# A masked softmax on one core: SyncE's first store waits for one more step of VectorE

## Chip, cores and metric

The kernel runs on one core of a Trainium2 chip. The metric is the device time of one execution in microseconds (us); the median of 3 runs of the kernel before is 156.31 us (156.23 to 156.35).

## What is computed

```python
def setup_inputs():
    batch, heads, seq_q, seq_k = 16, 8, 256, 256
    return {
        "x": np.random.randn(batch, heads, seq_q, seq_k).astype(np.float32),
        "lengths": np.random.randint(seq_k // 2, seq_k, size=batch).astype(np.int32),
    }

def reference(x, lengths):
    result = np.zeros_like(x)
    for b in range(batch):
        length = lengths[b]
        masked = x[b, :, :, :length].copy()
        masked = masked - np.max(masked, axis=-1, keepdims=True)
        exp_masked = np.exp(masked)
        result[b, :, :, :length] = exp_masked / np.sum(exp_masked, axis=-1, keepdims=True)
    return result.astype(np.float32)
```

It is a softmax over the last axis in which the columns from `lengths[b]` on are left out and come back as zeros. The input and the output are 33.55 MB each.

## The kernel before

**Tiles and slots.** One batch is one tile: 128 partitions with 16 rows (nt) of 256 columns each, 16 KB in a partition, 2 MB in all. SBUF holds 8 slots of this size (xt). There are 16 positions; positions 0, 1 and 2 hold batches 1, 2 and 3, position 3 holds batch 0, and from 4 on position and batch are the same (batch_of).

**Loads.** Position 0 is loaded from SyncE's queue in two halves (L136). Positions 1 and 2 are loaded whole from GpSimd's queue (L182). From position 3 on, GpSimd reads the batch's length into a register and picks the narrowest of some fixed widths that holds it (pick, L154): a narrow load, whose rows are 160 to 240 columns wide, or a whole one. Columns from 160 on were filled with zeros beforehand in the slots that get narrow loads (fill, L177). From position 4 on this is a loop, and a load there waits until the load two positions before has landed and until the slot's old tile is stored; so GpSimd has at most two of these loads out at a time.

**Compute.** For a tile, VectorE masks the columns from 128 on by a minimum with a ramp (mask, clip, L237; it raises the semaphore s_min), ScalarE does the exponential with the row's sum, 8 rows for each half tile (rows, L344; s_exp), and VectorE divides each half: a reciprocal of the 128x8 sums (L258) and a multiply (divide, L261; s_out). VectorE's order is written out by hand: both half masks of position 0, then for each position b the division of the first half, the mask of position b+1, the division of the second half. For b = 1 the mask of position 2 comes ahead of both divisions. So s_min is 2 after the two half masks of position 0, and 3 after the mask of position 1, which stands directly behind the division of the first half of position 0.

**Stores.** SyncE issues all stores in order (L143), in halves, quarters or whole tiles (parts). Each waits for the divisions that it covers (s_out); from position 2 on the first store of a position also waits until the stores of two positions before have landed (s_st).

**The end.** Behind the last division VectorE checks the row sums and TensorE counts the bad ones. With this input none is, and a second pass with subtracted maxima (L356 on) isn't run.

Of the kernel before, what the change touches and what calls it, by code (L numbers as in the profile page):

```python
# [21 lines left out]
def kernel(  # L22
# [6 lines left out]
    nc = tc.nc  # L29
# [18 lines left out]
    def batch_of(pos):  # L48
        return pos + 1 if pos < ahead else 0 if pos == ahead else pos
# [7 lines left out]
    def parts(b):  # L57


        if b == 0:  # L60
            cuts = [0, half, nt]
        elif b < 8:
            cuts = [0, half, half + quarter, nt]
        elif b < 13 or b == batch - 1:
            cuts = [0, half, nt]
        else:
            cuts = [0, nt]
        return [slice(i, j) for i, j in zip(cuts, cuts[1:])]
# [30 lines left out]
    with tc.tile_critical(no_gpsimd_drain=True):  # L99
# [11 lines left out]
        s_min = sem("s_min")  # L111
# [22 lines left out]
        for h in range(2):  # L134
            s = slice(h * half, (h + 1) * half)
            nc.sync.dma_start(out=xt[:, 0, s], in_=x_f[batch_of(0), :, s]).then_inc(s_ld[h], 16)  # L136
        for b in range(batch):
            s_b = s_st[b % 2]
            for s in parts(b):
                nc.sync.wait_ge(s_out, 2 * b + (s.stop - 1) // half + 1)  # L140
                if b >= 2 and s.start == 0:
                    nc.sync.wait_ge(s_b, 64 * (b // 2 + 1))
                nc.sync.dma_start(  # L143
                    out=out_f[batch_of(b), :, s, :], in_=xt[:, b % slots, s, :]
                ).then_inc(s_b, 16 * ((s.stop - s.start) // quarter))
# [262 lines left out]
```

## Time and profile before

| | |
|---|---|
| median of 3 runs | 156.31 us (156.23 to 156.35) |
| profiled execution: its time, its span | 156.43 us, 154.7 us |
| VectorE busy | 116.9 us (76%) |
| ScalarE busy | 105.5 us (68%) |
| GpSimd busy | 22.6 us (15%) |
| moved by DMA | 61.57 MB, 398 GB/s over the span |
| share of the 16 DMA engines | SyncE's queue (q1) 56.0%, GpSimd's (q0) 42.1% |
| HBM | 27.98 MB read, 33.55 MB written |

The span runs from the first to the last instruction; the time of the execution is 1.7 us longer. The DMA shares are the time that packets took, over 16 engines times the span. Engines are named as in the profile: DVE is VectorE, ACT is ScalarE, POOL is GpSimd, SP is SyncE; a small q behind a name is the engine's own queue of instructions that it issues. In the trace each DMA packet has a queue, a start, a duration and a size.

### The profile page before, as it was taken

The page shows a single profiled execution, that of the slowest core. Times are in us where ns is not written, and L with a number is a line of the kernel's source. Part 1 is how long each engine was busy: PE and PEld are TensorE (multiplying, and loading weights), DVE is VectorE, ACT ScalarE, POOL GpSimd, SP SyncE. Part 2 cuts the span into 40 slices and gives each one's busy share as a digit, 9 for nine tenths or more (in the row PEclk, how much of TensorE's full clock was granted, in tenths as well). Part 3 has the DMA queues.
Part 4 walks back from the last instruction along what each step waited for, and adds up shares of the span by engine and source line. Part 5 has one row for each costly group of instructions (what it writes and reads, how often), then busy time and mean ns, then how long its engine had stood idle before and what let it go on. Part 6 is the DMA issues. An engine that isn't in the chain of part 4 may idle for free.

```text
span 154.7 us, 1304 instructions
## 1 busy us (share of the span) xinstructions
PE 0.3 (0%) x2; PEld 0.2 (0%) x2; DVE 116.9 (76%) x91; ACT 105.5 (68%) x514; POOL 22.6 (15%) x30
## 2 busy tenths in 40 slices
PE   0000000000000000000000000000000000000000
PEld 0000000000000000000000000000000000000000
DVE  1349769996969696979979696969697686968500
ACT  3096889749595959688695959595968829596000
POOL 4994000100220200202030020220010000000000
DMA  4999999999999999999999999999999999999992
GB/s 121 420 430 436 273 420 416 379 410 441 414 401 391 423 406 421 409 415 421 393 421 410 411 415 401 419 411 421 415 419 417 437 430 415 432 447 415 434 417 95
DMA packets 10357, 61.57 MB, mean 398 GB/s; under 512 B 866, under 2 KB 978, under 8 KB 6642
## 3 DMA queue, kind: packets, MB, share of 16 engines
q1 hardware_dynamic: 5616, 35.65, 56.0%
q0 software_dynamic: 4736, 25.89, 42.1%
q14 instruction: 3, 0.02, 0.1%
q10 hardware_dynamic: 2, 0.00, 0.0%
HBM read 27.98 MB, written 33.55 MB: 398 GB/s over the span
## 4 chain that ended last, share of the span: by engine, by line
DMA 43%; DVE 29%; ACT 10%; issue 7%; ACTq 3%; POOL 1%; POOLq 1%; SPq 0%; PE 0%
DMA xt<-in_x_dram 23%; DMA out_dram<-xt 19%; DVE xt L261 15%; DVE xt L237 12%; ACT xt L344 10%; ACTq L344 3%; DVE inv_sum L258 1%; POOL xt L177 1%; DMA word<-in_lengths_dram 1%; DVE ends L293 0%; ACTq L350 0%; POOLq L126 0%; SPq L143 0%; DVE bad L296 0%; DVE len_s L228 0%
## 5 line engine op out<-in xcount | busy, mean ns | idle before, releaser
L344 ACT ACTIVATE xt<-xt (+1 forms) x256 | 102.4, 402 | 34.4 <-DVE xt L237 34.4
L261 DVE TENSOR_TENSOR xt<-xt,inv_sum 128x2048 f32<-128x2048 f32 x32 | 73.4, 2292 | 1.1
L344 ACT ACTIVATION_READ_ACCUMULATOR xt<-xt (+1 forms) x256 | 47.9, 187 | 0.0
L237 DVE SCALAR_TENSOR_TENSOR xt<-down,len_s,xt 128x2048 f32<-128x2048 f32 (+1 forms) x17 | 37.8, 2221 | 9.0 <-DMA xt<-in_x_dram 9.0
L154 POOL DMA_DIRECT2D xt<-in_x_dram x13 | 13.8, 1065 | 89.5 <-DMA out_dram<-xt 50.7
L258 DVE RECIPROCAL inv_sum<-row_sum 128x8 f32<-128x8 f32 x32 | 6.4, 199 | 15.9 <-ACT xt L344 15.9
L177 POOL MEMSET xt<- 128x1536 f32 x5 | 6.7, 1400 | 1.1 <-DVE len_s L228 1.1
L337 ACT ACT_TABLE_LOAD x1 | 1.3, 1283 | 1.6 <-SPq L99 1.6
L220 DVE TENSOR_SCALAR down<-iota_i 128x256 f32<-128x256 int32 x1 | 0.3, 301 | 1.6 <-POOL iota_i L167 1.6
L182 POOL DMA_DIRECT2D xt<-in_x_dram x2 | 1.2, 606 | 0.0
L293 DVE TENSOR_REDUCE ends<-row_sum 128x1 f32<-128x256 f32 x2 | 0.7, 411 | 0.0
L207 PE MATMUL count<-bad,ones_c 128*1 128x3 bf16 x1 | 0.2, 165 | 142.5 <-DVE bad L296 142.5
L225 DVE CAST len_b<-word 1x16 bf16<-1x16 int32 x1 | 0.2, 165 | 0.4 <-DMA word<-in_lengths_dram 0.4
L228 DVE TENSOR_SCALAR len_s<-len_f 128x16 f32<-128x16 f32 x1 | 0.2, 175 | 0.4 <-PE len_f L205 0.4
L167 POOL IOTA iota_i<- 128x256 int32 x1 | 0.3, 332 | 0.6 <-SPq L99 0.6
L304 DVE TENSOR_REDUCE redo<-count 1x1 f32<-1x3 f32 x1 | 0.1, 149 | 0.3 <-PE count L207 0.3
L296 DVE TENSOR_SCALAR bad<-ends 128x1 bf16<-128x1 f32 x3 | 0.3, 149 | 0.0
L173 POOL MEMSET seed<- 1x1 f32 x2 | 0.2, 226 | 0.0
L207 PEld LDWEIGHTS count<-bad,ones_c 128*1 128x1 bf16 x1 | 0.1, 79 | 142.6 <-DVE bad L296 142.6
L337 ACT ACTIVATE warm<-const-float32-0.0 128x1 f32<-128x1 f32 x1 | 0.2, 203 | 0.0
L170 POOL MEMSET ones<- 1x128 bf16 x1 | 0.2, 195 | 0.0
L205 PE MATMUL len_f<-len_b,ones 1*128 1x16 bf16 x1 | 0.2, 168 | 2.6 <-DVE len_b L225 2.6
(8 smaller groups left out, 0.8 us busy)
## 6 DMA issues: line engine op xcount, KB each, us to landing
out_dram<-xt SPq DMA_DIRECT2D x21, 1024.0 KB
xt<-in_x_dram POOLq DMA_DIRECT2D x4, 2048.0 KB, 14.3
out_dram<-xt SPq DMA_DIRECT2D x14, 512.0 KB
xt<-in_x_dram POOLq DMA_DIRECT2D x3, 1728.0 KB, 16.3
out_dram<-xt SPq DMA_DIRECT2D x2, 2048.0 KB
xt<-in_x_dram POOLq DMA_DIRECT2D x2, 1600.0 KB, 19.1
xt<-in_x_dram POOLq DMA_DIRECT2D x2, 1280.0 KB, 14.0
xt<-in_x_dram SPq DMA_DIRECT2D x2, 1024.0 KB, 6.4
```

Source lines behind the costliest of these rows:

```text
L154: nc.gpsimd.dma_start(out=xt[:, slot, :, :w], in_=x_n[:, b, :, :w]).then_inc(s_sw[par], 16)
L167: nc.gpsimd.iota(iota_i, pattern=[[1, seq_k]], base=0, channel_multiplier=0).then_inc(s_iota, 1)
L177: nc.gpsimd.memset(xt[:, b, :, low:], 0.0).then_inc(s_fill, 1)
L182: nc.gpsimd.dma_start(out=xt[:, b], in_=x_f[batch_of(b)]).then_inc(s_ld[b + 1], 16)
L207: nc.tensor.matmul(count, lhsT=ones_c, rhs=bad, start=True, stop=True).then_inc(s_count, 1)
L220: nc.vector.tensor_scalar(out=down, in0=iota_i, scalar1=0.5, scalar2=-big, op0=ALU.add, op1=ALU.mult)
L237: return nc.vector.scalar_tensor_tensor(out=t, in0=down[:, None, lo:hi].to_broadcast([P, s.stop - s.start, hi - lo]), scalar=len_s[:, batc ...
L258: step(nc.vector.reciprocal(out=inv_sum[:, b, s], in_=row_sum[:, b, s]))
L261: nc.vector.tensor_tensor(out=t, in0=t, in1=inv_sum[:, b, s, None].to_broadcast([P, half, seq_k]), op=ALU.mult,).then_inc(s_out, 1)
L293: step(nc.vector.tensor_reduce(out=ends[:, k : k + 1], in_=values, op=op, axis=AX))
L337: nc.scalar.activation(out=warm, in_=nc.const_aps.tensor(0.0, (P, 1), F32), func=EXP)
L344: ins = nc.scalar.activation(out=e, in_=e, func=EXP, accum_out=sum_h[:, i, j])
```

## The change

SyncE waits once, after the two loads of position 0 that it issues and ahead of its loop over stores, until s_min is at least 3, which is when VectorE has masked the tile of position 1. Nothing else is changed: the loads, whole and narrow, stay in GpSimd's queue, and each engine's instructions are the same and in the same order.

```diff
         for h in range(2):
             s = slice(h * half, (h + 1) * half)
             nc.sync.dma_start(out=xt[:, 0, s], in_=x_f[batch_of(0), :, s]).then_inc(s_ld[h], 16)
+        nc.sync.wait_ge(s_min, 3)
         for b in range(batch):
             s_b = s_st[b % 2]
             for s in parts(b):
```

## The prediction

> **What bounds the kernel now.** I read the page first, for the engines against the transfers. SyncE, VectorE and ScalarE all sit idle in every part of the span; the 16 DMA engines do not.
>
> ```profile
> span 154.7 us, 1304 instructions
> PE 0.3 (0%) x2; PEld 0.2 (0%) x2; DVE 116.9 (76%) x91; ACT 105.5 (68%) x514; POOL 22.6 (15%) x30
> DMA  4999999999999999999999999999999999999992
> GB/s 121 420 430 436 273 420 416 379 410 441 414 401 391 423 406 421 409 415 421 393 421 410 411 415 401 419 411 421 415 419 417 437 430 415 432 447 415 434 417 95
> ```
>
> The row of nines says that the DMA engines have work from the second slice to the last but one. The row below it says that the work goes at nearly one pace (400 to 440 GB/s), with one hole: the fifth slice (15.5 to 19.3 us), at 273 GB/s, while the busy digit stays at 9. In that slice the packets are slow, not missing. So this kernel ends when 61.57 MB have been moved. An edit that only reorders waits changes the time only by what it does to the pace of the packets, or by making the DMA engines run dry.
>
> Second, the view of stretches, cut where the pace changes (the last two columns are the DMA share and GB/s):
>
> ```profile
> 4.00:13.00 9.00, 0.00 (x0) 0.00 (x0) 4.61 (x4) 5.41 (x27) 8.11 (x8) 1.00 1.02 426
> 13.00:15.00 2.00, 0.00 (x0) 0.00 (x0) 1.85 (x2) 1.18 (x6) 0.45 (x1) 1.00 1.04 442
> 15.00:19.00 4.00, 0.00 (x0) 0.00 (x0) 3.37 (x3) 2.79 (x14) 0.72 (x1) 1.00 0.99 297
> 21.00:27.00 6.00, 0.00 (x0) 0.00 (x0) 5.93 (x5) 5.39 (x29) 0.00 (x0) 1.00 1.02 418
> 27.00:29.00 2.00, 0.00 (x0) 0.00 (x0) 1.97 (x3) 2.00 (x12) 0.00 (x0) 1.00 1.01 348
> 31.00:130.00 99.00, 0.00 (x0) 0.00 (x0) 82.92 (x58) 74.75 (x369) 10.94 (x10) 1.00 1.02 415
> 130.00:152.00 22.00, 0.17 (x1) 0.08 (x1) 13.31 (x16) 9.69 (x48) 0.00 (x0) 1.00 0.99 420
> ```
>
> Two slow stretches stand out, both with full queues. Stretch 1 (15 to 19) costs 4 x (1 - 297/426) = 1.21 us; stretch 2 (27 to 29) costs 2 x (1 - 348/418) = 0.33 us.
>
> Third, what happens just before them, in the timeline (SyncE, VectorE, GpSimd) and the DMA queues of short windows (q0 is GpSimd's queue with the loads, q1 SyncE's with the stores; packets, MB, share of the 16 engines):
>
> ```profile
> 13.48 5.32 SPq L143 DMA_DIRECT2D out_dram<-xt  x2
> 13.61 2.35 DVE L237 SCALAR_TENSOR_TENSOR xt<-down,len_s,xt 128x2048 f32<-128x2048 f32 x1 [0.15 <-DMA xt<-in_x_dram]
> 14.55 1.16 POOL L154 DMA_DIRECT2D xt<-in_x_dram  x1 [2.20 <-issue]
> 20.71 2.35 DVE L237 SCALAR_TENSOR_TENSOR xt<-down,len_s,xt 128x2048 f32<-128x2048 f32 x1 [2.31 <-DMA xt<-in_x_dram]
> ```
>
> ```profile
> q0 software_dynamic: 60, 0.88, 103.8%
> ...
> q0 software_dynamic: 30, 0.44, 75.4%
> q1 hardware_dynamic: 14, 0.11, 13.5%
> ...
> q0 software_dynamic: 174, 0.70, 101.2%
> q1 hardware_dynamic: 3, 0.00, 0.1%
> ```
>
> These are the windows 13 to 15, 17 to 19 and 27 to 29. In the packet records the first store, issued at 13.48, has a single packet before 17.8 and flows steadily only from 19. From 15.2 until then the loads' 16 KB packets, which took 0.61 us each before, take 1.0 to 1.3 us. In stretch 2 the pattern comes back: q1 has run dry at 26.9, the next store was issued at 25.53 (behind a multiply that ends at 25.50), its first packet runs at 29.0, and the loads' 4.8 KB packets take about 1.2 times their usual 0.19 us until then. So each time a store starts on an idle q1, the loads slow down from about 1.7 us after its issue to 3.5 to 5.6 us after it: by 30% (297 against 426) while a whole load is running, by 17% (348 against 418) while a narrow one is. Elsewhere q1 always has a backlog and there is no such stretch.
>
> **The change part by part.** One wait of SyncE is added, for s_min at 3. VectorE works in order: the first multiply of the first tile (which lets the first store go), then the mask of the second tile, which raises s_min to 3. That mask runs from 13.61 for 2.35 us, so the wait is over at 15.96 and the first store goes at about 15.99 in place of 13.48: 2.5 us later. The wait itself costs tens of ns, on an engine that only issues. Since the mask always stands behind that multiply, the wait cannot be met early; the change does what it says.
>
> What is queued behind it: all other stores. The second waits for a multiply that ends at 18.40, and is issued at 18.43, so it is not moved. Who waits for the first store: SyncE's first store of the third tile (issued at 30.41; the first tile's stores have landed by 27.95, 2.4 us of cover) and GpSimd's reuse of the first slot (load issued at 52.48, 24 us of cover). Both stay covered. What the DMA engines do in between: q0 holds the rest of the third tile's whole load, the fourth tile's narrow load (1.5 MB) and from 14.55 another narrow one (1.6 MB), over 8 us of work. They don't run dry. So the delay itself costs nothing; if that cover were gone it would cost up to 2.5 us.
>
> What it moves is the start-up of q1. Slowing begins 1.7 us after the issue: 17.7. The third tile's 2.1 MB start to flow at about 13.1 and need 4.9 us at 426 GB/s; undisturbed, they are through at about 18.0 to 18.5. So of the new stretch 0.3 to 0.8 us fall on the whole load (30%: 0.1 to 0.25 us), and the rest, until 3.5 to 5.6 us after the issue (19.5 to 21.6), on the narrow load (1.2 to 3.1 us at 17%: 0.2 to 0.5 us). The sum is 0.3 to 0.75 us; I take 0.5, since the end lies between two equally near rows. Against 1.21 this saves 0.7 us (0.45 to 0.9).
>
> Then stretch 2. The third tile now lands near 19.0 in place of 20.7, so its mask (at 20.71 after an idle 2.31) comes 1.7 us earlier, and the two multiplies behind it too, since ScalarE has their first half ready at 19.5. The store issued at 25.53 goes at about 23.8 and can flow 3.5 us later, at 27.3. q1's first two stores, 2 MB at the 260 to 275 GB/s that q1 gets beside a narrow load in the packet records of 20 to 26, end near 27.5. The gap closes or nearly so: 0 to 0.33 us saved; I take 0.2.
>
> Sum: 0.9 us off the profiled execution (156.43 us, of which 1.7 lie outside the span), 155.5. The median shown is 156.31, 0.12 below the profiled run; on it that makes 155.4. Does the gain reach the end? From 131 on only stores run, at 420 GB/s and with a backlog: the last store is issued at 144.16, could flow 3.5 us later, at 147.7, and comes to its turn at about 149; so VectorE and the issue have 1.3 us to spare, and the steps ahead of them move forward with the loads.
>
> Two rules of the Trainium skill bear on this. The row: the first store takes 3.5 to 4.4 us from issue to first packet. DMA: Bandwidth & Descriptors (Specifications) gives about 0.6 us for SyncE's path; by that the store would have been flowing at 14.1, and stretch 1 would have some other cause; the trace does not agree with 0.6 us here. The row: loads slow down beside a store that isn't yet moving. The same page (Back-pressure in remote DMA) says that stalled writes stall an engine's other queues too, which is told there of transfers between cores; it fits the row, and no run here yet shows that it is the cause.
>
> **The rivals.**
> *No change* (156.3). Stretch 1 is not the store's doing. GpSimd's narrow issue at 14.55 to 15.71, 0.6 us ahead of the first slow packet, is the other candidate, and it is not moved. Against it: the same issue at 38.31 falls on a whole load too, and 36 to 40 goes at 435 GB/s. Or the stretch moves with its whole price, 1.21 us for 1.21. The same page's rule (Issuing engines are not separate DMA queues) that the queues share the same engines and only interleave would give this result as well: the same bytes, the same time.
>
> *Slower* (157.0). The start-up stretch falls on the narrow load and is dearer there. The first narrow packets of stretch 1 (two of 4.6 KB, after 18.5) took about twice their usual time, as against 1.2 times in stretch 2. At twice, from 18.0 until 5.6 us after the issue (21.6), half of 3.6 us is lost, 1.8, with 0.2 for the end of the whole load: 2.0 in place of 1.21, less perhaps 0.1 of stretch 2: 0.7 slower, 157.0. It decides from a mean slowing of about 1.65 times over the 3.6 us (1.4 lost; with the 0.2, and 1.31 given back, 0.3 slower). Against it: only two packets showed it, the next four 1.25 times.
>
> *The start-up costs nothing any more* (154.8). With two stores issued 2.4 us apart and the whole load through, neither stretch is seen: 1.21 + 0.33 = 1.5 off. For it: every later store joins without a stretch; but all of those join a q1 that has work.
>
> **How the numbers follow.** My forecast 0.52, no change 0.20, slower 0.20, nothing lost 0.08. Its own range is the sum of the bounds, 0.45 to 1.2 off: 155.1 to 155.9. The range for all is 154.8 to 156.9, which leaves out half of the best case and about half of the worst, 0.14 in all. A measurement of this kernel can tell about 0.2%, 0.3 us. Nearly all of the forecast and the best case lie beyond it: faster 0.58; same 0.21; slower 0.21.
>
> **What would show it.** In the changed profile: the first store at about 16.0; the stretch 15 to 17.5 near 420 GB/s; a shallower hole between 17.7 and 21; the mask of the third tile at about 19.0, not 20.7; 27 to 29 above 348 GB/s; the last load and the last store earlier by the same amount. Wrong, if the hole stands at 15 to 19 although the store goes at 16.0 (then it is not the store's), if the hole moves and is as deep, or if a slice of the DMA row falls below 9 near 18.

## The result and the profile after

The changed kernel takes 155.64 us (median of 11 runs, 155.19 to 155.99) against 156.27 us for the kernel before (11 runs): ratio 0.9959, 95% interval 0.9946 to 0.9972, so 0.44 to 0.84 us faster. It is faster, by about two thirds of the 0.9 us that were forecast. The profiled execution took 155.27 us with a span of 153.6 us.

The page, with the same rows as before:

```profile
span 153.6 us, 1305 instructions
PE 0.3 (0%) x2; PEld 0.2 (0%) x2; DVE 116.9 (76%) x91; ACT 105.4 (69%) x514; POOL 22.6 (15%) x30
DMA  4999999999999999999999999999999999999993
GB/s 113 425 431 431 353 340 423 422 409 439 419 403 394 422 401 420 416 411 421 395 421 406 420 408 404 416 418 415 418 419 415 421 444 423 425 431 444 431 408 166
DMA packets 10357, 61.57 MB, mean 401 GB/s; under 512 B 866, under 2 KB 978, under 8 KB 6642
```

The work is the same to the packet (10357, 61.57 MB), and the DMA engines are as busy. The hole that filled the fifth slice now lies across the fifth and sixth (353, 340), and the eighth has gone from 379 to 422. The stretches, cut where the pace changes (last columns: DMA share, GB/s):

```profile
15.00:17.50 2.50, 0.00 (x0) 0.00 (x0) 2.47 (x3) 1.07 (x5) 0.73 (x1) 1.00 1.04 442
17.50:21.00 3.50, 0.00 (x0) 0.00 (x0) 2.61 (x2) 3.50 (x19) 0.00 (x0) 1.00 0.94 273
21.00:27.00 6.00, 0.00 (x0) 0.00 (x0) 5.90 (x7) 6.00 (x31) 0.00 (x0) 1.00 1.01 417
27.00:29.00 2.00, 0.00 (x0) 0.00 (x0) 2.00 (x1) 2.00 (x11) 0.00 (x0) 1.00 1.01 415
31.00:130.00 99.00, 0.00 (x0) 0.00 (x0) 81.77 (x58) 74.19 (x366) 10.91 (x10) 1.00 1.02 415
```

The first hole moved with the store and kept its depth: 3.5 x (1 - 273/430) = 1.28 us, where it was 1.21. The second one is gone: 415 where 348 stood. From 31 to 130 the pace is the same. The timeline (SyncE, VectorE) shows the steps that moved:

```profile
16.21 2.81 SPq L144 DMA_DIRECT2D out_dram<-xt  x2
19.51 2.35 DVE L238 SCALAR_TENSOR_TENSOR xt<-down,len_s,xt 128x2048 f32<-128x2048 f32 x1 [0.89 <-DMA xt<-in_x_dram]
```

The first store goes at 16.21. The third tile's mask starts at 19.51 in place of 20.71, and the store behind it at 24.33 in place of 25.53.

In the packet records the same can be counted: for every packet from 14.9 to 32 us, its duration above the usual one of its size (0.611 us for 16 KB, 0.309 for 8 KB, 0.178 for 4.6 KB, 0.185 for 4.8 KB, 0.162 for 4 KB), summed and divided by the 16 engines. (The 4.8 KB figure is low: beside stores 0.191 us is the commonest. With it every sum is 0.05 to 0.15 us smaller, and the differences between kernels move by 0.06 us at most.) That is 1.76 us before and 1.23 after, 0.53 less. Of this, 0.13 comes from the first hole (1.19 to 1.06) and 0.40 from the second (0.46 to 0.06). This count is called "lost" below.

The bytes say the same. Loads and stores had moved 10 MB at 28.03 us before and at 27.94 after, 11 MB at 30.74 and 30.37, and 61 MB at 150.67 and 150.21. So the lead is 0.09 us behind the first hole, 0.37 behind the second, and 0.46 near the end. The spans of the two profiled executions differ by more, 1.1 us: the rest arises behind 61 MB, where the last packet ends at 153.01 before and at 151.93 after.

### The profile page after: what moved, and what is told of

Its sections match the earlier page's. It is cut to its first block, busy times and chain, and to the rows that moved or that the text cites. A ratio compares the mean times of both kernels' runs of the same rounds, so it can differ in the third digit from the quotient of the medians.

```text
span 153.6 us, 1305 instructions
## 1 busy us (share of the span) xinstructions
PE 0.3 (0%) x2; PEld 0.2 (0%) x2; DVE 116.9 (76%) x91; ACT 105.4 (69%) x514; POOL 22.6 (15%) x30
## 2 busy tenths in 40 slices
DMA packets 10357, 61.57 MB, mean 401 GB/s; under 512 B 866, under 2 KB 978, under 8 KB 6642
## 4 chain that ended last, share of the span: by engine, by line
DMA 44%; DVE 29%; ACT 10%; issue 7%; ACTq 3%; POOL 1%; POOLq 1%; SPq 1%; PE 0%
DMA xt<-in_x_dram 23%; DMA out_dram<-xt 20%; DVE xt L262 15%; DVE xt L238 12%; ACT xt L345 10%; ACTq L345 3%; DVE inv_sum L259 1%; POOL xt L178 1%; DMA word<-in_lengths_dram 1%; SPq L144 1%; DVE ends L294 0%; ACTq L351 0%; POOLq L126 0%; DVE bad L297 0%; DVE len_s L229 0%
```

## The experiments

Each median is set against the kernel before, run on the same chip beside it (156.21 to 156.25 us).

**Where the holes come from.** The theory at the start was the prediction's: a store that starts on an idle SyncE queue slows the loads beside it. Four kernels bear on it.

*A later first store* (156.21 us, ratio 0.9995, 0.9985 to 1.0006):

```diff
-        nc.sync.wait_ge(s_min, 3)
+        nc.sync.wait_ge(s_min, 4)
```

> The changed kernel with its wait at s_min 4 in place of 3: the first store goes behind the mask of the third tile, at about 21 us in place of 16.2. Theory S (a store that starts on an idle SyncE queue slows the loads beside it from 1.7 us after its issue until its packets flow): 17.5 to 21 goes at about 425 GB/s, the hole moves on to about 22.8 to 26.5 and costs 1.0 to 1.3 us as before, no second hole; median 155.4 to 155.9, the same as the changed kernel within 0.3. Rival F (the hole belongs to a fixed moment of the opening): the hole stays at 17.5 to 21; same time. Rival D (waiting is dear once GpSimd's queue runs low, its next load being issued only behind the fourth tile's landing): a slice of the DMA row below 9 near 25, median 156.3 or more.

The store went at 21.86 and flowed from 25.6. The stretches:

```profile
15.00:17.50 2.50, 0.00 (x0) 0.00 (x0) 2.47 (x3) 1.22 (x7) 0.70 (x1) 1.00 1.01 429
18.60:22.00 3.40, 0.00 (x0) 0.00 (x0) 2.49 (x3) 3.40 (x19) 0.00 (x0) 1.00 1.04 328
22.00:25.00 3.00, 0.00 (x0) 0.00 (x0) 2.97 (x3) 3.00 (x16) 0.00 (x0) 1.00 1.02 337
26.00:30.00 4.00, 0.00 (x0) 0.00 (x0) 3.97 (x4) 3.15 (x16) 0.21 (x1) 1.00 1.08 445
```

None of the three theories holds. The slow stretch begins at 18.6, more than 3 us ahead of any store's issue, and is flat until the stores flow; the store's start adds nothing to it. What runs there is a narrow load by itself: its 4.6 KB packets take 0.234 us. The 4.8 KB packets of the narrow load behind it take 0.23 us until the stores flow, and 0.19 from then on. Whole loads by themselves go at 429. So a **narrow load alone is slow**, at 328 to 337 GB/s. The second hole of the kernel before (27 to 29, 348 GB/s, q0 alone) is this, and no start of a store.

*The second hole put back* (156.03 us, ratio 0.9989, 0.9972 to 1.0005), on the changed kernel:

```diff
                 nc.sync.wait_ge(s_out, 2 * b + (s.stop - 1) // half + 1)
+                if b == 0 and s.start:
+                    nc.sync.wait_ge(s_out, 3)
```

> The changed kernel, with its second store held until s_out is 3, which is when the first multiply of the second tile is done (about 24.3 in place of 18.65), so that SyncE's queue runs dry once more at about 24.5 and starts again at about 27.8. Theory S: a second hole of 0.3 to 0.4 us comes back at about 26 to 28 while the first one is as in the changed kernel: median 155.9 to 156.1, 0.3 to 0.4 above the changed kernel; so the second hole's closing is most of what the change gained. Rival E (the gain came from somewhere else, such as the end): 155.6, unchanged.

```profile
17.50:21.00 3.50, 0.00 (x0) 0.00 (x0) 2.67 (x2) 3.50 (x19) 0.00 (x0) 1.00 0.94 265
25.50:27.50 2.00, 0.00 (x0) 0.00 (x0) 1.97 (x3) 2.00 (x12) 0.00 (x0) 1.00 1.03 353
```

With SyncE's queue made to run dry, the second hole is back at 353 GB/s beside an unchanged first one, and 0.4 us of the gain are gone, as was expected. That closing the second hole is most of the gain is shown; by the bytes too, since here 11 MB had been moved at 30.71, within 0.03 us of the kernel before.

*Whole loads on SyncE's queue* (156.01 us, ratio 0.9981, 0.9969 to 0.9993), on the kernel before:

```diff
+        for b in range(1, ahead):
+            nc.sync.dma_start(out=xt[:, b], in_=x_f[batch_of(b)]).then_inc(s_ld[b + 1], 16)
         for b in range(batch):
             s_b = s_st[b % 2]
...
-        for b in range(1, ahead):
-            nc.gpsimd.dma_start(out=xt[:, b], in_=x_f[batch_of(b)]).then_inc(s_ld[b + 1], 16)
```

> The kernel before, with the two whole loads of positions 1 and 2 issued from SyncE's queue ahead of the stores in place of GpSimd's queue. SyncE's queue then has work until about 18 to 21 us, and the first store, issued at 13 to 16, stands behind the loads in a queue that is not idle. Theory S: no hole near its start, 1.2 us saved: 155.0, up to 0.5 more if the narrow load of position 3 delays the tiles ahead of it. Rival W (the price is paid when the first writes mix into the reads, whichever queue carries them): the hole stays, with its 1.2 us, 156.3.

```profile
17.50:19.00 1.50, 0.00 (x0) 0.00 (x0) 1.50 (x1) 1.48 (x7) 0.00 (x0) 1.00 1.02 363
19.00:22.00 3.00, 0.00 (x0) 0.00 (x0) 0.71 (x1) 3.00 (x17) 0.00 (x0) 1.00 0.98 321
```

The first store, issued at 13.63, stood behind two loads in a queue that was never idle, and flowed from 21. The hole stays, directly ahead of it, with 16 KB packets of up to 1.5 us. An idle queue is not what it takes. Of what was gained, the packets put 0.1 us into the first hole and 0.2 into the time from 26 us on; the narrow load of position 3 had company from its first packet at 10.6 us on, but what each part owes to that was not tried.

*A small store early* (156.57 us, ratio 1.0028, 1.0019 to 1.0038), on the kernel before; zero is a tile of zeros, and the last tile's store waits for s_early:

```diff
+        nc.sync.wait_ge(s_zero, 1)
+        nc.sync.dma_start(out=out_f[batch - 1, :, nt - 1, :], in_=zero).then_inc(s_early, 16)
```

> The kernel before, with one more small store: zeros, 128 rows of 1 KB, to a part of the output that the last tile's store writes again; it is issued right behind the first two loads, so it goes through at about 8 us. It adds 128 KB, 0.3 us of all DMA engines. Theory S: SyncE's queue is idle again from about 8 to 13.5, and the hole at 15 to 19 stays with its price: 156.5 to 156.7. Rival T (the first store of an execution is dear for being the first, 1.2 us against 0.35 for the second start): the hole at 15 to 19 shrinks to 0.3 to 0.5 us: 155.6 to 155.9.

```profile
15.00:19.00 4.00, 0.00 (x0) 0.00 (x0) 3.81 (x3) 2.35 (x12) 0.73 (x1) 1.00 0.97 334
27.00:29.00 2.00, 0.00 (x0) 0.00 (x0) 1.97 (x3) 2.00 (x11) 0.00 (x0) 1.00 1.04 348
```

The hole at 15 to 19 stands, though shallower: 4 x (1 - 334/426) = 0.86 us, where it was 1.21. The one at 27 to 29 is unchanged, and the time is 0.35 us longer, about what the added bytes cost (0.3). So most of the price is not one that an execution pays for its first store. Why the hole is 0.35 us shallower here, and why the time doesn't show it, stays open.

**What the first hole needs.** A narrow load alone explains the second hole, but not 16 KB packets of 0.61 us that become 0.9 on average, single ones 1.3, nor the changed kernel's 4.6 KB packets of 0.27 to 0.31 us (means of half a microsecond) at 18.5 to 20.

*Both first stores together* (155.96 us, ratio 0.9982, 0.9967 to 0.9996):

```diff
-        nc.sync.wait_ge(s_min, 3)
+        nc.sync.wait_ge(s_out, 2)
```

> The changed kernel with its wait at s_out 2 in place of s_min 3: the first two stores go together, at about 18.65, and can flow from about 22.3. From 18 until then the narrow load of position 3 runs alone. Theory N (a narrow load alone runs at 315 to 335 GB/s, 4.6 KB packets at 0.234 us, against 0.18 us beside stores) with no extra cost of the store's start: 18 to 22 flat at about 320 GB/s, about 0.25 lost of 4.3 us, 1.0 us. Theory Q (a store's start costs extra, packets up to 0.30 us, as long as GpSimd's queue holds more than one load behind it): 20.3 to 22.3 at about 260 GB/s. Median 155.7 by N alone, 156.2 by N and Q.

```profile
18.60:22.00 3.40, 0.00 (x0) 0.00 (x0) 2.71 (x4) 3.40 (x18) 0.00 (x0) 1.00 1.04 329
```

Issued at 18.72 and 19.19, the stores cost nothing of their own: 0.234 us a packet from 19 until they flow. Lost: 1.34 us. The time lies between the two forecasts.

*One load queued* (160.49 us, ratio 1.0279), on the changed kernel:

```diff
         nc.gpsimd.wait_ge(s_fill, slots - ahead)
+        nc.gpsimd.wait_ge(s_sw[1], 16)
```

> The changed kernel, with GpSimd's load of position 4 held until the load of position 3 has landed (about 22), so that GpSimd's queue holds one load, not two, when the first store starts. Theory Q (the extra slowing at 18.5 to 20.5 comes from what is queued on GpSimd's side): packets stay at 0.234 us until the stores flow, 320 GB/s in place of 270. Rival P (the extra comes with the first store of an execution, whatever is queued): 0.27 to 0.31 us as in the changed kernel. GpSimd's queue then runs dry from about 22 to 26, where the stores alone go at about 420 GB/s, so the time is 155.2 to 155.6 by Q, 155.6 to 156.0 by P.

The packets at 18.5 to 20 still take 0.27 to 0.29 us on average, so what is queued on GpSimd's side is not the cause. The time was expected 4.5 us lower or more: all later loads trail, the last ends at 138.9 in place of about 131, and the DMA engines run dry near the end:

```profile
140.00:146.00 6.00, 0.00 (x0) 0.00 (x0) 5.97 (x4) 4.12 (x22) 0.00 (x0) 1.00 0.58 246
```

*Position 3 whole* (156.54 us, ratio 1.0019, 1.0003 to 1.0035), on the changed kernel:

```diff
-        pick(v_len, 0, ahead, 1, [160, 176, 192, 208, 224, seq_k])
+        pick(v_len, 0, ahead, 1, [seq_k])
```

> The changed kernel with position 3 loaded whole in place of narrow: 0.56 MB more are read (2.0 MB for 1.5 MB), 1.3 us of all DMA engines at 425 GB/s. Theory N: 18 to 20 loses what the narrow load lost for being alone, and only the store's start is left there; of the 1.3 us some 0.4 to 0.5 us come back: 156.4 to 156.6. Rival (the hole is the store's alone, and dearer on a whole load, as in the kernel before): 1.2 us stay in the hole, 156.9 or more.

```profile
17.50:20.00 2.50, 0.00 (x0) 0.00 (x0) 1.78 (x2) 2.50 (x13) 0.00 (x0) 1.00 0.97 321
```

Of the 1.2 us that 512 KB more cost at 425 GB/s, 0.9 show against the changed kernel: lost fell from 1.23 to 0.95. The stretch 17.5 to 20 still goes at 321 GB/s, with no narrow load in it; that part belongs to the store.

*The same kernel again* (155.93 us, one run):

> The changed kernel unaltered, one more profile: whether the hole at 17.5 to 21 comes back with the same depth. All theories: about 273 GB/s there; time 155.2 to 156.0. If the depth differs by more than 20 GB/s, part of the run-to-run spread (155.19 to 155.99) is the depth of this hole.

17.5 to 21 went at 266 GB/s, against 273. The hole is stable, and it is not what makes this kernel's runs differ by 0.8 us. The two traces of the kernel show where they part: 61 MB had been moved at 150.21 us in one and at 150.20 in the other, but the last packet ends at 151.93 and at 152.57. Behind 151.72 the slower one has only three packets left, each of which starts as the one before ends. That is the 0.6 us between their spans; the other executions have no trace, and why the end varies stays open.

*The first store in two quarters*, on the changed kernel (155.71 us, ratio 0.9949, 0.9932 to 0.9967) and on the kernel before (155.70 us, ratio 0.9954, 0.9938 to 0.9970):

```diff
         if b == 0:
-            cuts = [0, half, nt]
+            cuts = [0, quarter, half, nt]
```

> The changed kernel, with the first store of position 0 cut in two quarters, which are issued one behind the other at 16.0 and 16.4. Theory P (the packets of 0.27 to 0.31 us come where one store waits alone on an idle queue; with a second one right behind it, as in the runs whose first two stores went together, only the narrow load's own 0.234 us is left): 18 to 20 at about 315 GB/s and flow from 19.7; 0.4 to 0.7 us less lost: 155.0 to 155.3. Rival A (it comes with any first store that is issued before some 18 us): as the changed kernel, 155.5 to 155.8.

> The kernel before, its first store cut in two quarters, issued at 13.5 and 13.9. Theory P: the whole load at 15 to 18 keeps 0.61 us a packet, flow from about 17.2; 1.0 us or more saved at the first hole, the second hole (27 to 29, a narrow load alone) stays: 155.2 to 155.5. Rival A: the hole at 15 to 19 stays, 156.2.

In the changed kernel 17.5 to 21 goes at 283 GB/s; in the kernel before, 15 to 19 at 320, with 16 KB packets of up to 1.2 us. A second store right behind the first does not take the extra away. The kernel before gained 0.55 us all the same. By the packets some 0.25 of it is a shallower first hole, and the rest is the second hole, which closed: 27 to 29 goes at 418. The stores' 4 KB packets take turns with the load's (some 25 of each in half a microsecond at 20 us), and so the stores last longer. Neither beats the changed kernel.

*One store, late* (155.76 us, ratio 0.9968, 0.9956 to 0.9980), on the kernel of the pair:

```diff
                 nc.sync.wait_ge(s_out, 2 * b + (s.stop - 1) // half + 1)
+                if b == 0 and s.start:
+                    nc.sync.wait_ge(s_min, 4)
```

> The kernel of the pair (first store at 18.7), with the second store held until the mask of the third tile, about 21.0, so that the first one waits alone on the idle queue. Theory P: packets of 0.27 to 0.31 us at 20 to 22, 0.4 us more lost than with the pair: 156.3 to 156.4. Rival A: flat 0.234 us from 18.6 until the store flows, as with the pair: 155.9 to 156.0.

```profile
18.60:22.00 3.40, 0.00 (x0) 0.00 (x0) 2.51 (x3) 3.40 (x18) 0.00 (x0) 1.00 1.01 323
```

Flat at 323 GB/s until the store flows: no extra, though it waits alone. So it is the moment or what runs then, not the company.

*The pair beside a whole load* (156.61 us, ratio 1.0022, 1.0006 to 1.0038), the kernel of the pair with position 3 whole:

```diff
-        pick(v_len, 0, ahead, 1, [160, 176, 192, 208, 224, seq_k])
+        pick(v_len, 0, ahead, 1, [seq_k])
```

> The kernel of the pair (first two stores at about 18.7) with position 3 loaded whole, so that a whole load runs from 18 to 24 when the stores start. In all runs so far with extra slowing the first store was issued while a whole load was running, before about 18 us; in the three without it, after both. Theory W (a store that starts while a whole load runs slows the loads): packets of 0.7 to 1.0 us in place of 0.61 at 20 to 23, 0.7 to 1.0 us lost, median 156.4 to 156.8. Rival T (it belongs to the first 18 us, whatever runs): 0.61 us a packet until the stores flow, nearly nothing lost, 155.6 to 155.9; and since a whole load alone needs no stores beside it, this would also show that the 0.234 us of the pair's run came from the narrow load.

```profile
15.00:19.00 4.00, 0.00 (x0) 0.00 (x0) 3.62 (x3) 2.60 (x14) 0.00 (x0) 1.00 0.99 416
20.50:22.50 2.00, 0.00 (x0) 0.00 (x0) 1.97 (x3) 2.00 (x12) 0.00 (x0) 1.00 1.05 287
24.00:27.00 3.00, 0.00 (x0) 0.00 (x0) 2.93 (x5) 3.00 (x17) 0.00 (x0) 1.00 1.00 422
```

The stores go at 18.69, as in the pair's run, and with a whole load running the extra is there: 0.95 us a packet on average, from 1.8 us after the issue until they flow at 23. So the extra goes with **a store that starts while a whole load runs**, wherever that is put; beside a narrow load it is absent (three runs with issues at 18.7 to 21.9).

**The account.** Lost, against the kernel before's 1.76, and the measured differences of the medians:

| kernel | lost, difference | median, difference |
|---|---|---|
| changed | -0.53 | -0.63 |
| later first store | +0.02 | -0.01 |
| second hole put back | -0.08 | -0.19 |
| whole loads on SyncE's queue | -0.34 | -0.21 |
| pair | -0.42 | -0.29 |
| one store, late | -0.44 | -0.49 |
| quarters on the changed kernel | -0.69 | -0.54 |
| quarters on the kernel before | -0.61 | -0.55 |

The kernels that are not in this table move other bytes, were out of loads, or ran once. The two columns agree within 0.15 us, so slow packets between 15 and 32 us carry the difference; the lead in bytes, 0.37 us at 11 MB and 0.46 at 61 MB, says the same. Where the bytes differ the count is rougher: with some 0.3 us for the added bytes the small store early should have cost 0.05 us by it (lost 1.50), and cost 0.35; with 1.2 us the two kernels with position 3 whole (lost 0.95 and 1.14) should have cost 0.4 and 0.6, and cost 0.3 and 0.4.

## Why the prediction was right, and where it was not

- **The bound** was right. The time followed what the packets lost, and the one run in which the DMA engines did run dry, one load queued, was 4.2 us slower than the kernel before.
- **The wait and what stands behind it** were right: the store 2.7 us later (2.5 forecast; the step ahead of the wait was 0.2 us later in this execution), the second store at 18.65 for 18.43 by the same 0.2, no slice below 9 but the first and the last. One sign failed without harm: the last load didn't end earlier (131.2 us for 130.7), nor was the last store issued earlier (144.7 for 144.2).
- **The store's start moves the first hole**: right, and GpSimd's issue, which stayed at 14.56, is not its cause. The step that failed is its price on the narrow load. The 17% came from 27 to 29 and was read as a store's start beside a narrow load; the runs show it to be the narrow load without stores, which begins when SyncE's queue runs dry at 27.0; that this is 1.5 us after an issue was chance. The start, begun beside the end of the whole load, kept its price: 0.13 us saved (by the stretches, nothing), where 0.7 were forecast. That is the second branch of the no-change rival, a hole that moves with its whole price, and one of the prediction's own signs of being wrong: for the first hole both came true.
- **The second hole** closed for the reason given: third tile and next store 1.2 us earlier (1.7 forecast), q1 not dry. The term was mis-sized from the other side: 0.33 by the stretches and 0.40 by the packets, where 0.2 was taken.
- **The sum**: 0.53 by the packets against 0.9 forecast; the rest of the measured 0.63 is inside the interval. The total came out nearer than its terms, because their errors went opposite ways: the larger term, 0.7 of the 0.9, was nearly all missing, and the smaller one came in double. That the time lies in the forecast range is in good part luck.
- **Two readings of the kernel before** were off. The 16 KB packets from 15.2 to 19 took 0.9 us on average, not 1.0 to 1.3 each; and a stretch of 1.8 to 3.9 us less 0.3 to 0.8 leaves 1.0 to 3.6 us on the narrow load, not 1.2 to 3.1. The sum moves by about 0.1 us at most.
- **The slower rival** had half of a point: the packets were dearer than 1.2 times (0.27 to 0.31 us, 1.5 to 1.75 times), near the 1.65 that it needed, but for 2 us, not 3.6.
- **The skill's rules.** The Trainium skill (DMA: Bandwidth & Descriptors, Issuing engines are not separate DMA queues) says that DMAs from different engines run on the same 16 DMA engines and interleave. Read as the no-change rival read it, the same bytes would have taken the same time; they took 0.63 us less, because what runs beside what changes the pace. The 0.6 us from issue to first byte (the Trainium skill, same page, Specifications) did not hold either: the first store took 3.4 to 4.6 us, and 7.6 in the run where it stood behind two loads.

## What to carry to other kernels

Where the DMA engines never idle, look for slices that are busy and slow, and ask of each packet size how long it takes alone and beside the other queue. A stretch with one queue empty has two suspects, the start of the other queue and the load that is left alone; move the start far away (the later first store) before pricing either. A delay was free here only as long as it made no queue run dry: it cost 0.4 us in the run with the second hole put back, and over 4 us with one load queued.

## What the hardware showed unexpectedly

- Narrow loads (768-byte rows) run alone at 328 GB/s, 0.234 us for 4.6 KB, and at 0.18 us a packet with stores beside them; whole loads, whose packets are 16 KB, need no company (429 GB/s). The Trainium skill (DMA: Bandwidth & Descriptors, Specifications) gives 512 bytes as the smallest transfer for full rate; the measurement with 768 differs.
- A store that starts while a whole load runs slows the load's packets from 0.61 to about 0.8 to 1.1 us (medians of one microsecond; single ones up to 1.6) until its own flow, and the narrow packets right behind it to about 0.3. Why stays open. The queue's being idle, the store's company and what GpSimd has queued are excluded; its being the first store is not the whole of it.
